# Moving the ones products of gate and branch weights further behind their squares, and one block's squares further behind its load

## The chip, the cores and the metric

The kernel runs on one core of one Trainium2 chip. The metric is the device time of one execution in microseconds (us). Below, PE is the matrix engine, PEld its weight loads, DVE, ACT and POOL the vector, scalar and general engines, SP the engine that issues the transfers. L247 is line 247 of the kernel before.

## What is computed

One layer of an encoder block on x of 1024 tokens by 1024 features, float32 in and out:

```python
u = rms_norm(x, norm1_g)
q, k, v, cb, cc, ch, ga, gb = split(u @ w_in)              # 512 wide each, ga and gb 1024
y_a = neighbourhood_attention(rms(q), rms(k), v, rpb) @ w_attn_branch    # 512 -> 1024
y_b = (cb * conv3(cc * ch, conv_w)) @ w_conv_branch                      # 512 -> 1024
m = sigmoid(ga) * y_a + sigmoid(gb) * y_b
x = x + m @ w_o
h = rms_norm(x, norm2_g) @ w_mlp_in
x = x + square(relu(h)) @ w_mlp_out
```

## The kernel before, in words

**Numbers.** Every float32 matrix is split into two float16 halves, a high part (ACT, a scaled copy) and a low part (DVE, `scalar_tensor_tensor`, the remainder), and a product is made of three matmul passes (high by high, high by low, low by high). Each block of weights is brought to a power of two first, so it needs the sum of squares of the whole block before it can be split.

**How that sum is made.** Four steps on three engines: ACT squares the block and accumulates per partition (L326 for the blocks of `w_attn_branch`, L1411 for the gates, L1434 for `w_conv_branch`; a gate block's halves are multiplied by the norm's gains first, four copies each, L1224); ACT copies the sums into columns of a tile called `ones` (L241, `summed`); PE adds over the partitions with two or four tiny matmuls against a matrix of ones (L247, `all_sum`), called the *ones product* below; DVE turns the result into a power of two (L250, then L518 to L525). After that the split can start (ACT L390 or L1360, DVE L377 or L1364).

**Stages.** The change lies in the stage after attention, 300 to 560 us into the execution. PE works there on *units*: a unit is 12 matmuls of 128x512 into one PSUM bank (6 for the conv branch). The gates ga and gb are made in blocks S1 to S7 by seven products in place of eight (a Strassen-like scheme): seven units each, with weights in the tile `w_s`. Weights A0 to A3 (`w_wa`) and B0 to B3 (`w_wb`) are the four column blocks of the two branch matrices; `ab(j)` is the run of units that multiplies Aj and Bj. The order on PE is: first gate unit, A0, S1, `ab(0)`, S2, S3, `ab(1)`, S4, S5, `ab(2)`, S6, `ab(3)`, S7, then `w_o`. A name in the trace such as `ps_s<-uT,w_s` is a gate unit, `bT,w_wb` a conv branch unit, `qD,w_wa` an attention branch unit.

**What sets the order.** The program is written out by Python generators that run side by side: one emits the PE units, others prepare the coming weight blocks. Each emission of a unit lets the others take some steps. Each engine then runs its own instructions strictly in the order of emission, PE too: a ones product whose column isn't there yet holds up all the units behind it. Two helpers hold a generator back. `apart(mark, n * 6144, work)` waits until n units have been emitted since the mark, so it sets how many units lie between the squares and the ones product. `aged(ch, i, n)` waits until n units after the transfer of a block was issued before the squares are emitted. PSUM banks come from three tags (3 banks d, 3 s, 2 o) by the letters "dsodsods" in turn (`anybank`); the ones products take a bank from the same turn, so a ones product that is moved also changes the bank letters of the units behind it.

**After a gate block.** DVE combines the seven products in PSUM (L1524 to L1546 for one half, L1613 to L1628 for the other), so a bank stays taken until DVE has read it. The four sums of quarter blocks that S blocks need (`gsum`, L1348) are made by POOL, between the combination's own products (L1604). ACT L1493 and L1501 and DVE L1504 turn a finished block of the merged result into its float16 halves.

Of the kernel before, what the change touches and what calls it, by code (L numbers as in the profile page):

```python
# [101 lines left out]
def encoder_block(ctx: ExitStack, tc: tile.TileContext, x, weights, cols, gqk, rel, masks, out):  # L102
# [105 lines left out]
    late, units, forced, side, splitting = [], [0], [False], [False], [False]  # L208
    work, spent, pace = [0], [0], [0]

    def apart(mark, n=3, of=units):
        while of[0] < mark + n and not forced[0]:
            yield WAIT
# [89 lines left out]
    class Chunk:  # L303
# [11 lines left out]
        def prep(self):  # L315
            n = len(self.widths)
            nk = sum(k for k, _ in self.widths)
            rm, a, b, s = (cols_of("prep", i) for i in (nk, 1, 1, 1))
            self.inv = keep()
            tot = sum(k * w for k, w in self.widths)  # L320
            if self.kind == "A" and self is not cA[0]:
                while not self.raw or not aged(self, 0):
                    yield WAIT
                sm = cols_of("prep", 4)
                for i in range(4):
                    A.activation(M[0][:, 7, :256].bitcast(BF16), self.raw[0][:, 256 * i:256 * i + 256], AF.Square,  # L326
                                 scale=sc[:, at(self.rows, i)], accum_out=sc[:, at(sm, i)])
                c = summed(sm)
                yield
                yield from apart(work[0], 3 * 6144, work)  # L330
                yield from all_sum(c, b, anybank(), 1e-36)
                yield from pow2_half(b, 14, s, self.inv)
            elif self.kind in "QKCG":
                self.parts = wsp.tile([128, 2, tot], F16, name="w16_ws", tag="ws")
                for p, (k, w) in enumerate(self.widths):
                    while len(self.raw) <= p:
                        yield WAIT
                    A.activation(self.parts[:, 1, :k * w].bitcast(BF16), self.raw[p][:, :k * w], AF.Square,
                                 accum_out=sc[:, at(rm, p)])
                    yield  # L340
                V.tensor_reduce(sc[:, a], sc[:, at(rm, 0, n)], axis=AX, op=OP.add)
                c = ones_col()
                V.tensor_tensor(c, sc[:, a], sc[:, gm2], op=OP.mult)
                yield from apart(units[0], {"Q": 2, "C": 2, "K": 1}.get(self.kind, 3))
                yield from all_sum(c, b, bank(self.bank) if self.bank else anybank(), 1e-36)
                yield from pow2_half(b, 14, s, self.inv, more=self.more)
            else:
                yield from self.largest(rm, a, b)
                yield from pow2(b, 14, s, self.inv, False, more=self.more)
            V.tensor_scalar(sc[:, rm], sc[:, self.rows], sc[:, s], None, op0=OP.mult)  # L350
            yield
            while done[0] < self.first or self.tag not in wpool:
                yield WAIT
            if self.half is not None:
                if not self.half:
                    vhome.append(wsp.tile([128, 2, 2, tot], F16, name="w16_v", tag="ws"))
                self.parts = vhome[0][:, self.half]
            elif self.kind not in "QKCG":
                self.parts = wpool[self.tag].tile([128, 2, tot], F16, name="w16_" + self.tag, tag=self.tag)
            f = o = 0  # L360
            todo = []
            for p, (k, w) in enumerate(self.widths):
                todo.append((p, [(i * w, w, rm.start + o + i) for i in range(k)], f))
                f += k * w
                o += k
            prev, scaled = None, {}
            for it in todo + [None]:
                if prev:
                    p, parts, f = prev
                    if self.fine:  # L370
                        assert not self.pool
                    for o, m, c in [] if self.fine else parts:
                        hi, lo = (self.parts[:, w, f + o:f + o + m] for w in range(2))
                        if p in self.pool:
                            G.tensor_tensor(lo, scaled[p][:, o:o + m], hi, op=OP.subtract)
                        else:
                            V.scalar_tensor_tensor(lo, self.raw[p][:, o:o + m], sc[:, c:c + 1], hi,  # L377
                                                   op0=OP.mult, op1=OP.subtract)
                    done[0] += 1
                    load_upto(done[0] + 5)  # L380
                splitting[0] = True
                if it:
                    p, parts, f = it
                    if p in self.pool:
                        scaled[p] = w1p.tile([128, 1024], F32, name="scaled", bufs=1)
                        for o, m, c in parts:
                            G.tensor_scalar(scaled[p][:, o:o + m], self.raw[p][:, o:o + m], sc[:, c:c + 1], 1.0,
                                            op0=OP.mult, op1=OP.mult)
                    for o, m, c in parts:
                        A.activation(self.parts[:, 0, f + o:f + o + m], self.raw[p][:, o:o + m], AF.Copy,  # L390
                                     scale=sc[:, c:c + 1])
                    if self.fine:
                        yield
                        for o, m, c in parts:
                            V.scalar_tensor_tensor(self.parts[:, 1, f + o:f + o + m], self.raw[p][:, o:o + m],
                                                   sc[:, c:c + 1], self.parts[:, 0, f + o:f + o + m],
                                                   op0=OP.mult, op1=OP.subtract)
                            if o + m < self.widths[p][0] * self.widths[p][1]:
                                yield
                prev = it  # L400
                self.split = it is None
                yield
# [32 lines left out]
    for (kind, j), pieces in plan():  # L435
        ch = chunks[kind, j] = Chunk(kind, [(nk, sum(n for _, n in cs)) for _, _, nk, cs in pieces],
                                     {"A": "wa", "B": "wb"}.get(kind, "ws"), rows.get(kind, lambda j: g1)(j),
                                     j if kind == "V" else None, 9 if kind in "VQKCGS" else 0)
        ch.first = len(loads)
        for p, (k, w) in enumerate(ch.widths):  # L440
            ch.offs.append(offset)
            if kind != "X" and (kind, j) != ("1", 0) and (kind, j, p) != ("1", 1, 1):
                loads.append((ch, p))
            offset += 128 * k * w
    cG, cS = chunks["G", 0], {n: chunks["S", n] for n in range(1, 8)}
    cV, cConv, cA, cB, cO, c1, c2, c2x = ([chunks[k, j] for j in range(n)] for k, n in
                                              (("V", 2), ("C", 4), ("A", 4), ("B", 4), ("O", 2),
                                               ("1", 16), ("2", 4), ("X", 4)))
# [756 lines left out]
    def scale_of(am, more, n=3):  # L1205

        a, mark = am
        yield from apart(mark, n * 6144, work)
        b, s, inv = cols_of("prep", 1), cols_of("prep", 1), keep()
        yield from all_sum(a, b, anybank(), 1e-36)  # L1210
        yield from pow2_half(b, 14, s, inv, more)
        return s, inv

    def aged(ch, i):
        return forced[0] or i >= len(ch.when) or work[0] >= ch.when[i] + (4 if ch is cS[2] else 2) * 6144

    def rows_scaled(ch, g):

# [181 lines left out]
    def prep_s(n):  # L1400

        ch = cS[n]
        if n == 1:
            while ch.s is None:
                yield WAIT
            s = ch.s
        else:
            yield from rows_scaled(ch, g1)
            sm = cols_of("prep", 2)
            for i in range(2):  # L1410
                A.activation(M[0][:, 7].bitcast(BF16), ch.raw[i], AF.Square, accum_out=sc[:, at(sm, i)])  # L1411
                yield
            c = summed(sm)
            s, ch.inv = yield from scale_of((c, work[0]), 9, 3)
        while done[0] < ch.first or n > 1 and not cS[n - 1].split or gates[0] < n - 1:
            yield WAIT
        t = w3p.tile([128, 4, 512], F32, name="gsum", bufs=1)
        yield from forms_sum(ch, t, None)
        ch.P = wsp.tile([128, 7, 2, 512], F16, name="w16_s", tag="ws")
        yield from forms_split(ch, t, s, ch.P, n == 1, n > 1)  # L1420
        ch.split = True
# [248 lines left out]
    for j in range(4):  # L1670
        if j < 3:
            n = 2 * j + 1
# [11 lines left out]
        n = 2 * j + 2  # L1684
# [666 lines left out]
```

## Time and profile before

| | |
|---|---|
| median of 3 runs | 1209.42 us (1209.11 to 1210.09) |
| profiled execution | 1211.59 us |
| its span in the trace | 1209.8 us |
| PE busy | 1192.8 us, 99% |
| DVE, ACT, POOL busy | 78%, 65%, 40% |
| chain that ended last | PE 61%, DVE 4%, ACT 2%, DMA 2% |

The profiled execution is 2.2 us above the median and contains 1.8 us outside its span. All times of the trace are microseconds from the start of the span. In a timeline row stand the start, the length, the engine, the line, the operation with output and inputs, the count, and in brackets the idle time before it with what ended it. In a row of windows stand, for each engine, its busy time and number of instructions, then the granted PE clock (PEclk, 1.00 is full), the share of time of the DMA engines and GB/s.

### The profile page before, as it was taken

The page shows a single profiled execution, that of the slowest core. Times are in us where ns is not written, and L with a number is a line of the kernel's source. Part 1 is how long each engine was busy: PE and PEld are TensorE (multiplying, and loading weights), DVE is VectorE, ACT ScalarE, POOL GpSimd, SP SyncE. Part 2 cuts the span into 40 slices and gives each one's busy share as a digit, 9 for nine tenths or more (in the row PEclk, how much of TensorE's full clock was granted, in tenths as well). Part 3 has the DMA queues.
Part 4 walks back from the last instruction along what each step waited for, and adds up shares of the span by engine and source line. Part 5 has one row for each costly group of instructions (what it writes and reads, how often), then busy time and mean ns, then how long its engine had stood idle before and what let it go on. Part 6 is the DMA issues. An engine that isn't in the chain of part 4 may idle for free.

```text
span 1209.8 us, 17188 instructions
## 1 busy us (share of the span) xinstructions
PE 1192.8 (99%) x6267; PEld 575.7 (48%) x6267; DVE 947.9 (78%) x1767; ACT 785.8 (65%) x1278; POOL 480.9 (40%) x314
## 2 busy tenths in 40 slices
PE   8999999999989899999999999999999999999998
PEld 7444444455434344444458444444444444444444
DVE  7987877898777677877888655455448989999998
ACT  8774668778777664436778777677675854746440
POOL 5610020221434440411004765565557562564572
PEclk9999999999989899999999999999999999999999
DMA  7755546687684425325196455345375925435202
GB/s 261 194 157 120 114 98 134 138 159 132 162 278 157 151 76 174 95 97 210 28 173 177 163 191 190 126 164 191 123 269 191 349 104 182 166 109 222 104 36 105
DMA packets 168374, 189.63 MB, mean 157 GB/s; under 512 B 123616, under 2 KB 124128, under 8 KB 164192
## 3 DMA queue, kind: packets, MB, share of 16 engines
q1 hardware_dynamic: 168288, 188.52, 51.7%
q8 instruction: 49, 0.80, 0.3%
q14 instruction: 37, 0.30, 0.1%
HBM read 117.19 MB, written 41.42 MB: 131 GB/s over the span
## 4 chain that ended last, share of the span: by engine, by line
PE 61%; DVE 4%; ACT 2%; DMA 2%; issue 1%; POOL 0%; SPq 0%; DVEq 0%
PE ps_d L256 23%; PE ps_s L256 21%; PE ps_o L256 16%; DMA raw<-in_weights 1%; DVE w_s L1364 1%; DMA x<-in_x 1%; DVE mL L1504 0%; DVE sc L409 0%; ACT raw L1224 0%; ACT mH L326 0%; ACT sg L1535 0%; DVE sc L1701 0%; ACT mH L1411 0%; ACT mL L1493 0%; DVE w_wb L1364 0%
## 5 line engine op out<-in xcount | busy, mean ns | idle before, releaser
L256 PEld LDWEIGHTS <-ops 128*128 128x128 f16 x1356 | 132.4, 98 | 157.3
L256 PEld LDWEIGHTS <-w 128*128 128x128 f16 x1368 | 132.9, 98 | 139.4
L1189 PE MATMUL ps_d<-uT,w_ws 128*128 128x512 f16 x576 | 127.9, 379 | 0.0
L256 PE MATMUL ps_s<-ops 128*128 128x512 f16 (+1 forms) x528 | 119.7, 377 | 0.0
L256 PE MATMUL ps_d<-ops 128*128 128x512 f16 x480 | 110.1, 379 | 0.0
L2172 ACT ACTIVATE ops<-hf,sc 128x2048 f16<-128x2048 f32 x26 | 52.0, 1998 | 84.8 <-PE ps_s L256 37.7
L1348 POOL TENSOR_TENSOR tsum<-raw 128x512 f32<-128x512 f32 x28 | 48.2, 1738 | 139.5 <-DVE v L1800 74.0
L1750 POOL TENSOR_TENSOR as<-as 128x512 f32<-128x512 f32 x60 | 82.9, 1381 | 41.7 <-ACT as L2032 38.2
L256 PEld LDWEIGHTS <-w_s 128*128 128x128 f16 x588 | 57.5, 99 | 69.9 <-issue 4.1
L1189 PEld LDWEIGHTS <-w_ws 128*128 128x128 f16 x576 | 54.5, 98 | 65.2 <-issue 1.0
L256 PE MATMUL ps_d<-u2T,w 128*128 128x512 f16 (+1 forms) x360 | 78.8, 368 | 0.0
L256 PE MATMUL ps_o<-ops 128*128 128x512 f16 (+1 forms) x348 | 78.6, 375 | 0.0
L2174 DVE SCALAR_TENSOR_TENSOR ops<-hf,sc,ops 128x2048 f16<-128x2048 f32 x26 | 73.8, 2837 | 3.2 <-ACT ops L2172 2.2
L256 PE MATMUL ps_o<-u2T,w 128*128 128x512 f16 (+1 forms) x348 | 76.0, 368 | 0.0
L256 PE MATMUL ps_s<-u2x,w 128*128 128x512 f16 (+1 forms) x336 | 74.5, 371 | 0.0
L1224 ACT ACTIVATE raw<-raw,sc 128x256 f32<-128x256 f32 x164 | 67.8, 494 | 1.6 <-DMA raw<-in_weights 1.6
L1377 ACT ACTIVATE w<-raw,sc 128x512 f16<-128x512 f32 (+1 forms) x28 | 24.6, 927 | 51.1 <-DVE sc L524 51.1
L2065 DVE TENSOR_TENSOR as<-ps_s,as 128x512 f32<-128x512 f32 x13 | 9.0, 692 | 57.9 <-ACT as L2084 57.9
L2188 POOL TENSOR_TENSOR raw<-raw 128x1024 f32<-128x1024 f32 x8 | 30.8, 3873 | 37.3 <-DVE ops L2182 37.3
L256 PEld LDWEIGHTS <-mH 128*128 128x128 f16 x304 | 29.6, 98 | 30.8 <-issue 0.3
L2178 ACT ACTIVATE ops<-raw,sc 128x1024 f16<-128x1024 f32 x24 | 26.3, 1139 | 26.7 <-DVE sc L152 19.2
L256 PE MATMUL ps_d<-u2x,w 128*128 128x512 f16 (+1 forms) x204 | 43.0, 360 | 0.0
(444 smaller groups left out, 2717.5 us busy)
## 6 DMA issues: line engine op xcount, KB each, us to landing
raw<-in_weights SPq DMA_DIRECT2D x89, 512.0 KB, 5.6
hs<-as SPq DMA_DIRECT2D x16, 1792.0 KB, 8.1
hf<-hs SPq DMA_DIRECT2D x26, 1024.0 KB, 6.5
bT<-bf SPq DMA_DIRECT2D x28, 512.0 KB, 4.4
w2x<-in_weights SPq DMA_DIRECT2D x16, 512.0 KB, 7.8
raw<-in_weights SPq DMA_DIRECT2D x16, 384.0 KB, 3.7
xt<-in_x SPq DMA_DIRECT2D x8, 512.0 KB, 10.8
gs<-s SPq DMA_DIRECT2D x4, 1024.0 KB, 4.4
```

Source lines behind the costliest of these rows:

```text
L256: T.matmul(ps, l, r, start=a, stop=b)
L1189: T.matmul(ps, l, r, start=a, stop=b)
L1224: A.activation(v, v, AF.Copy, scale=sc[:, at(g, 4 * i + k)])
L1348: G.tensor_tensor(t[:, o], a, b, op=OP.add)
L1364: V.scalar_tensor_tensor(o(1), w, sc[:, get(n)], o(0), op0=OP.mult, op1=OP.subtract)
L1377: A.activation(o(0), w, AF.Copy, scale=sc[:, scale(n)])
L1750: sub.tensor_tensor(z[o], z[a], z[b], op=op)
L2065: V.tensor_tensor(z[5], ps[6], z[4], op=OP.add)
L2172: A.activation(P[:, 1, 0], hf, AF.Copy, scale=sc[:, Rs])
L2174: V.scalar_tensor_tensor(P[:, 1, 1], hf, sc[:, Rs], P[:, 1, 0], op0=OP.mult, op1=OP.subtract)
L2178: A.activation(P[:, 0, 0, 1024 * i2:1024 * i2 + 1024], w[i2], AF.Copy, scale=sc[:, fw])
L2188: G.tensor_tensor(w11[i2], w11[i2], w12[i2], op=OP.add)
```

## The change

Three delays are set anew; no arithmetic is changed.

- `Chunk.prep`, kind A (blocks A1, A2, A3): the squares used to be emitted as soon as the block was loaded; now two units after the load was issued, and for A1 seven units after. The ones product follows six units after the squares in place of three.
- `prep_s` (S2 to S7): the ones product follows the squares by 4, 3, 4, 5, 6 and 6 units in place of 3 for all.
- `aged` gets the number of units as a parameter; other blocks keep 2, and S2 keeps 4. The conv branch (`prep_b`) keeps its distances.

```diff
@@ Chunk.prep
-                while not self.raw or not aged(self, 0):
+                while not self.raw or not aged(self, 0, 7 if self is cA[1] else 2):
                     yield WAIT
...
                 c = summed(sm)
                 yield
-                yield from apart(work[0], 3 * 6144, work)
+                yield from apart(work[0], 6 * 6144, work)
                 yield from all_sum(c, b, anybank(), 1e-36)
...
-    def aged(ch, i):
-        return forced[0] or i >= len(ch.when) or work[0] >= ch.when[i] + (4 if ch is cS[2] else 2) * 6144
+    def aged(ch, i, n=2):
+        return forced[0] or i >= len(ch.when) or work[0] >= ch.when[i] + (4 if ch is cS[2] else n) * 6144
...
@@ prep_s
             c = summed(sm)
-            s, ch.inv = yield from scale_of((c, work[0]), 9, 3)
+            s, ch.inv = yield from scale_of((c, work[0]), 9, {2: 4, 3: 3, 4: 4, 5: 5}.get(n, 6))
```

ACT in S1, before the change: A1's four squares and their copy (L326, L241) stand between the copies of S2's first half (L1224) and the conversion of the conv branch (L966).

```order
L1224 ACTIVATE raw<-raw,sc 128x2x128 x4
L326 ACTIVATE mH,sc<-raw,sc 128x256 x4
L241 ACTIVATE ones<-sc 128x4
L966 ACTIVATE mH<-bT 128x512 x2
L1518 ACTIVATE sg<-raw 128x512
L1515 ACTIVATE sg<-ps_s,sc 128x512
```

The same squares on ACT after the change:

```order
L1411 ACTIVATE mH,sc<-raw 128x1024 x2
L241 ACTIVATE ones<-sc 128x2
L1224 ACTIVATE raw<-raw,sc 128x2x128 x4
L1546 ACTIVATE sg<-ps_s 128x512
L1360 ACTIVATE w_wb<-raw,sc 128x2x128 x4
L326 ACTIVATE mH,sc<-raw,sc 128x256 x4
L241 ACTIVATE ones<-sc 128x4
L1360 ACTIVATE w_s<-raw,sc 128x512
```

A1's squares have moved behind the squares of S2 (L1411 and the first L241) and the second part of B0's split (L1360 to w_wb).

ACT in S2 before the change, where the splits of S3's weights (L1360), the squares of S4 (L1411, L241) and the conversion of the merged block (L1501) meet:

```order
L1546 ACTIVATE sg<-ps_o 128x512
L1360 ACTIVATE w_s<-raw,sc 128x512
L1360 ACTIVATE w_s<-raw,sc 128x2x512
L1411 ACTIVATE mH,sc<-raw 128x1024 x2
L241 ACTIVATE ones<-sc 128x2
L1360 ACTIVATE w_s<-gsum,sc 128x2x512 x2
L1501 ACTIVATE mH<-mH,sc 128x1024
```

The same place on ACT after the change:

```order
L1546 ACTIVATE sg<-ps_o 128x512
L1360 ACTIVATE w_s<-gsum,sc 128x2x512 x2
L1224 ACTIVATE raw<-raw,sc 128x2x128 x4
L1411 ACTIVATE mH,sc<-raw 128x1024 x2
L241 ACTIVATE ones<-sc 128x2
L1501 ACTIVATE mH<-mH,sc 128x1024
```

The copies of S4's second half (L1224), its squares and its copy now stand between the split of the quarter sums (`w_s<-gsum`) and L1501; before, they stood ahead of that split.

PE at S5's ones product, before the change: it stands inside `ab(1)`, between two conv branch units.

```order
L256 LDWEIGHTS w_wb
L256 MATMUL ps_d<-bT,w_wb 128x512
L247 LDWEIGHTS ones
L247 MATMUL ps_s<-ones 128x1
...
L256 LDWEIGHTS w_wb
L256 MATMUL ps_o<-bT,w_wb 128x512
```

And after the change:

```order
L256 LDWEIGHTS w_wa
L256 MATMUL ps_o<-qD,w_wa 128x512
L247 LDWEIGHTS ones
L247 MATMUL ps_d<-ones 128x1
...
L256 LDWEIGHTS w_s
L256 MATMUL ps_s<-uT,w_s 128x512
```

It now stands behind the last unit of `ab(1)` and ahead of the first unit of S4. The other ones products move on PE in the same way: S2's from behind four units of S1 (after the first gate unit) to behind five, A1's from behind the first of them to the end of `ab(0)`'s attention units.

## The prediction

> **What bounds the kernel now.** I read the page first, then the waits of PE, then PE's timeline around each wait, and last the timelines of the engines that end the waits.
>
> ```profile
> PE 1192.8 (99%) x6267; PEld 575.7 (48%) x6267; DVE 947.9 (78%) x1767; ACT 785.8 (65%) x1278; POOL 480.9 (40%) x314
> PE ps_s L247 <- ACT ones L241: 7.3, 2, 3.7
> PE ps_d L247 <- ACT ones L241: 1.8, 1, 1.8
> ```
>
> PE is busy 99% of the span, so a change that leaves its matmuls alone can only win what PE waits, or what it runs at a lower clock. The two largest waits of the list are both for the copies that feed ones products, 9.1 us in three places. The timeline shows the first two:
>
> ```profile
> 326.25 2.75 PE L256 MATMUL ps_s<-uT,w_s 128*128 128x512 f16 x12
> 330.84 0.24 PE L247 MATMUL ps_d<-ones 128*128 128x1 bf16 x4 [1.83 <-ACT ones L241]
> ...
> 336.12 2.75 PE L256 MATMUL ps_d<-uT,w_s 128*128 128x512 f16 x12
> 342.61 0.19 PE L247 MATMUL ps_s<-ones 128*128 128x1 bf16 x2 [3.74 <-ACT ones L241]
> 342.82 5.28 PE L256 MATMUL ps_o<-qD,w_s 128*128 128x512 f16 x12
> ...
> 350.75 2.75 PE L256 MATMUL ps_s<-s4T,w_s 128*128 128x512 f16 x12
> 353.34 1.46 PE L256 MATMUL ps_d<-bT,w_wb 128*128 128x512 f16 x6
> ```
>
> A1's product (x4) stands one unit behind 326.25 and waits 1.83 us; S2's (x2) waits 3.74 us, and the unit behind it lasts 5.28 us. A unit has 2.75 us in its row, but the next starts 2.59 us behind its start (350.75 to 353.34), so I step PE by 2.59 for 12 matmuls and 1.30 for 6, and a wait as the trace counts it begins 0.16 us behind the step. The third wait is S5's product, in the middle of `ab(1)`:
>
> ```profile
> 391.05 2.75 PE L256 MATMUL ps_o<-uT,w_s 128*128 128x512 f16 x12
> ...
> 413.16 1.46 PE L256 MATMUL ps_d<-bT,w_wb 128*128 128x512 f16 x6
> 418.22 0.19 PE L247 MATMUL ps_s<-ones 128*128 128x1 bf16 x2 [3.60 <-ACT ones L241]
> 418.27 2.72 PE L256 MATMUL ps_o<-bT,w_wb 128*128 128x512 f16 x6
> ...
> 426.03 1.46 PE L256 MATMUL ps_o<-bT,w_wb 128*128 128x512 f16 x6
> ```
>
> Between 418.27 and 426.03 stand 7.76 us for two half units and a whole one, 5.18 at the normal step: 2.6 us lost to the clock, on top of the wait. After the second wait it is 350.75 less 342.82, 7.93 for two units of 5.18: 2.75 us. The windows show the clock itself:
>
> ```profile
> 327.90:331.30 3.40, 1.57 (x12) 0.68 (x10) 3.26 (x6) 3.27 (x12) 0.00 (x0) 1.00 0.42 95
> 338.20:341.60 3.40, 0.67 (x4) 0.19 (x2) 2.17 (x7) 3.37 (x8) 1.62 (x2) 1.00 1.05 405
> 341.60:348.40 6.80, 5.76 (x16) 2.08 (x16) 3.70 (x4) 4.60 (x12) 6.45 (x6) 0.50 1.02 378
> 413.30:416.70 3.40, 1.32 (x7) 0.49 (x5) 3.37 (x7) 3.40 (x8) 0.28 (x1) 1.00 1.04 419
> 416.70:423.50 6.80, 5.28 (x15) 1.97 (x15) 1.68 (x8) 4.97 (x8) 5.92 (x5) 0.50 0.53 181
> ```
>
> The first figure behind the comma is PE's busy time, the last but two the clock. Two stretches of 6.8 us ran at 0.50. The 3.4 us ahead of them held 0.67 and 1.32 us of PE work. The 3.4 us around the wait of 1.83 held 1.57 us and nothing dropped. So in this trace the drop lies between 1.57 and 1.32 us of work in such a stretch.
>
> **The change, part by part.**
>
> *A1's product.* It goes behind the attention units of `ab(0)`, and its squares go with it, off ACT's list in S1. With `ab(0)` from 350.7 (below), three half units and two whole ones ahead of it, it stands at 359.8, 29 us later. The 1.83 us go at that place. Its new cover is the work of S2's split and B0's on ACT, ahead of it by then.
>
> *S2's product.* It moves by one unit only: five units behind 326.25 is 339.20. What feeds it is not made earlier:
>
> ```profile
> 336.76 0.22 DVE L1439 TENSOR_SCALAR sc<-sc 128x2 f32<-128x2 f32 x1
> 337.01 1.49 ACT L1360 ACTIVATE w_wb<-raw,sc 128x128 f16<-128x128 f32 x4 [2.02 <-DVE sc L1439]
> 338.41 1.69 ACT L1224 ACTIVATE raw<-raw,sc 128x256 f32<-128x256 f32 x4
> 342.35 0.20 ACT L241 ACTIVATE ones<-sc 128x2 bf16<-128x2 f32 x1
> 330.00:340.00 10.00, 8.03 (x40) 3.59 (x40) 9.76 (x24) 7.95 (x19) 0.17 (x1) 1.00 0.74 238
> ```
>
> ACT idles 2.02 us for DVE L1439, and DVE is busy 9.76 of 10 us there (third pair of figures), with the same instructions in the same order as before. A1's squares taken off ACT therefore only lengthen that idle time; L241 stays at 342.35. PE arrives at 339.2, 339.4 by the row's end, and waits about 3.3 us. I let the clock drop as before. Since one unit more is done ahead of the wait, the rest of S1 ends 2.6 us sooner, `ab(0)` starts at 350.7 and S2 at 365.1 (it was 367.64).
>
> *The squares of S4's second half.* They and their copies move, on ACT, from ahead of the split of the quarter sums to behind it, and so ahead of L1501. Behind L1501 hangs DVE, and behind DVE a PSUM bank:
>
> ```profile
> 366.49 0.69 DVE L1617 TENSOR_TENSOR zb<-ps_s,zb 128x512 f32<-128x512 f32 x1 [1.10 <-PE ps_s L256]
> 369.27 1.42 DVE L1593 SCALAR_TENSOR_TENSOR sg<-zb,sc,sg 128x512 f32<-128x512 f32 x2
> 370.10 1.71 POOL L1604 TENSOR_TENSOR mH<-sg 128x512 f32<-128x512 f32 x1 [10.49 <-DVE sg L1593]
> 382.26 1.15 ACT L1360 ACTIVATE w_s<-gsum,sc 128x1024 f16<-128x1024 f32 x1 [2.48 <-POOL gsum L1348]
> 383.32 1.13 ACT L1501 ACTIVATE mH<-mH,sc 128x1024 f16<-128x1024 f32 x1
> 385.53 1.27 DVE L1504 SCALAR_TENSOR_TENSOR mL<-mH,sc 128x1024 f16<-128x1024 f32 x1
> 388.89 0.69 DVE L1527 TENSOR_TENSOR sg<-ps_d,sg 128x512 f32<-128x512 f32 x1
> ```
>
> The chain runs from L1593 over POOL's products and quarter sums to ACT's last split, L1501, L1504, the four additions to L1527. Before, L1527 read a d bank that nothing waited for. With the letters shifted it reads the o bank that S3's third unit needs next. Working: DVE L1617 no longer waits 1.10 us for PE but for its own list, which now has A1's scale and split in it; I put L1593 at 368.0, 1.3 earlier. The bounds of this are 2.6 earlier (all of PE's gain) and 1.1 later (no gain, and the six small steps of A1's scale put in ahead, each at most the 0.22 us of L1439). The inserted work is 4.05 us: L1224, L1411 and L241 of S2 go from 338.41 to 342.46. L1501 then starts at 383.32 - 1.3 + 4.05 = 386.1, L1504 at 387.1, L1527 ends 4.05 us later (385.53 to 389.58 before) at 391.2. PE is at that unit at 365.1 + 9 x 2.59 + 0.1 = 388.5. It waits 2.5 us (from 388.7, the end of the row) and starts at 391.2, where the row of before has 391.05. The 2.6 us won in S1 are gone: 0.15 lost in all.
>
> *What the clock makes of that wait.* Bounds: nothing (the wait of 1.83 us cost no clock) and 2.64 us (the waits of 3.60 and 3.74). 2.5 us lies about midway between 1.83 and 3.60. The windows say the same: 2.5 us of idle time wholly inside a stretch of 3.4 leaves 0.9 us of work, enough for a drop, but split evenly over two it leaves 2.1 in each, and where the stretches fall is not tied to the program. I take half, 1.3 us.
>
> By the Trainium skill, "TensorE: Matmul & The Clock Gate", HAM oscillation, the rule is no idle gaps over about 3.4 us. By that rule this wait would cost no clock. The two drops here followed waits of 3.74 and 3.60 us, which agrees, but the second was split, with 2.1 us of it in the stretch ahead of the drop, so the trace does not bear out the limit as a length of one gap.
>
> *S5's product.* It goes from the seventh place in `ab(1)` to its end:
>
> ```profile
> 410.04 2.00 ACT L1535 ACTIVATE sg<-sg,sc 128x2048 f32<-128x2048 f32 x1 [7.56 <-DVE sg L1533]
> 417.96 0.20 ACT L241 ACTIVATE ones<-sc 128x2 bf16<-128x2 f32 x1
> ```
>
> From S3's third unit at 391.2 come five units (12.95), 0.1 for A2's product, and `ab(1)` with seven half units and four whole ones (19.4): 423.65. Its copy is ready at 418.1, 5.5 us ahead; the cover is gone only if ACT's 410.04 slips by more than that. So the wait of 3.60 and the 2.64 us of clock go: 6.24 us.
>
> *The other products* (S3, B1, S4, A2, B2 to S7). None of S3's, B1's, S4's or A2's waits over 0.2 us before. Worked through with the shifted starts, S3's copy is at 362.2 with PE at 363.7, B1's at 375.0 against 375.4, S4's at 386.1 against 385.9: up to 0.2 us, which would come off the wait behind it. B0's low part, the cover of `ab(0)`, has its end at 349.2:
>
> ```profile
> 346.00 3.29 DVE L1364 SCALAR_TENSOR_TENSOR w_wb<-raw,sc,w_wb 128x256 f16<-128x256 f32 x4
> 450.00:540.00 90.00, 89.84 (x420) 40.70 (x419) 68.23 (x137) 42.56 (x67) 18.28 (x15) 1.00 0.33 103
> 540.40 7.38 DMA x<-in_x
> ```
>
> From 450 to 540 ACT is busy 42.56 of 90 us, so the later products, one to three units further back, keep their cover; I cost them at nothing. The chain of waits passes at 540.40 to a transfer; it follows PE's last gate unit, so it moves with PE and the gain is not lost there.
>
> **Sum.** -6.24 + 0.15 + 1.3 = -4.8 us. The profiled execution, 1211.59 us (span 1209.8 and 1.8 around it), would become 1206.8; it stands 2.2 us above the median of 1209.42, which becomes 1204.6.
>
> **The rivals.**
>
> *A wait without a drop, always.* Same waits, but 2.5 us never costs clock: -6.1, 1203.3 us. For it speaks that no wait under 3.6 us has cost clock here; against it the 1.32 us of work, in a stretch that dropped. This is also the time that the Trainium skill's rule of 3.4 us gives.
>
> *No wait at S3's third unit.* If L1527 ends at 388.7 or sooner, because the chain is 3.8 us earlier than before in place of 1.3 or ACT makes up the 4.05 us, the 2.6 us of S1 stay: -6.24 - 2.6, 1200.6 us. Against it: POOL's and ACT's rows from 370.10 to 383.32 have hardly a gap that could close.
>
> *The wait grows.* If L1593 comes 1.1 us later than before in place of 1.3 earlier, L1527 ends at 393.6, PE waits 4.9 us and the clock drops, as at 3.60: -6.24 + 2.55 + 2.64 = -1.05, 1208.4 us, no change that can be told. For it speaks that DVE is almost full and that A1's split (waiting for ACT) now stands ahead of L1617.
>
> *Slower: S4's second half is loaded late.* A1's raw weights are held till their split, now about 365.5 in place of 361, and the buffer goes to that half of S4.
>
> ```profile
> raw<-in_weights SPq DMA_DIRECT2D x89, 512.0 KB, 5.6
> ```
>
> It should land at 371; ACT wants it at 382.0. Each us after that delays L1501 and PE by one. With the drop the gain left is 3.4 us, so slower by 0.2% begins at a landing of 388, four times the 5.6 us of the row; 10 us late would be about 1216 us. The row speaks against it.
>
> *That the change does not do what it says* holds for S2's product, in the likeliest case already: its distance grows, its wait stays.
>
> **How the numbers follow.** The likeliest case, a wait of about 2.5 us at S3's third unit that costs some clock, 0.50: 1204.6, its own range 1203.3 to 1206.0. No drop 0.20, no wait 0.12, the grown wait 0.11, the late load 0.07. The range goes from 1200.5 (no wait) to 1207.8 (a wait some 2 us longer) and leaves out the late load and most of the grown wait. 0.2% is 2.4 us, about what a measurement of this kernel can tell from no change: the first three cases are faster, 0.82; the grown wait is the same, 0.11; the late load slower, 0.07.
>
> **What would show it.** Right: no wait at A1's product (four matmuls, behind the attention units of `ab(0)`); S2's product waiting 3.3 us till 342.6, with a unit of some 5 us behind it; S3's third unit waiting 2 to 3 us for DVE L1527 till about 391.2; no wait at S5's product, about 423.7, and PE ahead by some 5 us at `w_o`. Wrong: S2's copy earlier than 342 (then DVE was not the limit); L1501 at 383 or earlier; a wait for a ones copy or for weights in S4 to S7; or ACT waiting for a transfer near 382.

## The result and the profile after

The changed kernel takes 1206.25 us (median of 9 runs, 1205.51 to 1206.69) against 1209.38 us of the kernel before on the same chip (1207.37 to 1211.60); the ratio is 0.9973, with a 95% interval of 0.9963 to 0.9983. So 3.1 us are won, where 4.8 were forecast (1204.6 us, range 1200.5 to 1207.8). The profiled execution took 1206.47 us, its span is 1204.7 us.

The first row of the page:

```profile
PE 1189.0 (99%) x6267; PEld 573.9 (48%) x6267; DVE 952.2 (79%) x1767; ACT 786.8 (65%) x1278; POOL 480.0 (40%) x314
```

PE is busy 3.8 us less with the same 6267 matmuls: fewer of them ran at half clock (the mean granted clock is 0.997, before 0.994). PE's timeline in S1 to S5:

```profile
342.71 0.19 PE L247 MATMUL ps_s<-ones 128*128 128x1 bf16 x2 [3.25 <-DMA bf<-mL]
342.93 4.11 PE L256 MATMUL ps_o<-uT,w_s 128*128 128x512 f16 x12
...
349.47 1.46 PE L256 MATMUL ps_s<-bT,w_wb 128*128 128x512 f16 x6
...
358.53 0.24 PE L247 MATMUL ps_s<-ones 128*128 128x1 bf16 x4
...
376.45 0.19 PE L247 MATMUL ps_d<-ones 128*128 128x1 bf16 x2 [2.07 <-ACT ones L241]
376.51 4.39 PE L256 MATMUL ps_s<-uT,w_s 128*128 128x512 f16 x12
380.73 2.75 PE L256 MATMUL ps_d<-qD,w_s 128*128 128x512 f16 x12
...
391.14 2.75 PE L256 MATMUL ps_o<-uT,w_s 128*128 128x512 f16 x12
...
423.62 0.19 PE L247 MATMUL ps_d<-ones 128*128 128x1 bf16 x2
423.67 2.75 PE L256 MATMUL ps_s<-uT,w_s 128*128 128x512 f16 x12
```

A1's product (four matmuls, now at 358.53) no longer waits. S2's waits 3.25 us till 342.71; the row puts that down to a transfer of a tile that this product doesn't read, and what ended it is ACT's copy, below, which is done at 342.66. S5's doesn't wait, and S4 starts at 423.67, where it was 429.91. New is a wait of 2.07 us at 376.45, at B1's product, with 1.6 us of clock behind it (380.73 less 376.51 is 4.22, not 2.59). S3's third unit starts at 391.14; before it was 391.05. A smaller new wait, 1.31 us at 529 us, is shown further down. What ended these waits, on ACT and DVE:

```profile
342.46 0.20 ACT L241 ACTIVATE ones<-sc 128x2 bf16<-128x2 f32 x1
371.01 1.06 ACT L1493 ACTIVATE mL<-mH 128x1024 bf16<-128x1024 f32 x1 [5.78 <-POOL mH L1604]
372.85 1.76 ACT L1360 ACTIVATE w_s<-raw,sc 128x512 f16<-128x512 f32 x2 [0.69 <-DVE sc L524]
376.20 0.20 ACT L241 ACTIVATE ones<-sc 128x2 bf16<-128x2 f32 x1
385.68 1.13 ACT L1501 ACTIVATE mH<-mH,sc 128x1024 f16<-128x1024 f32 x1
...
390.22 0.69 DVE L1527 TENSOR_TENSOR sg<-ps_o,sg 128x512 f32<-128x512 f32 x1
```

B1's squares now stand behind L1493, which waits for POOL, and behind a split that waits for DVE, so their copy is done at 376.3. L1527, which frees the bank that S3's third unit needs, ends at 390.9.

### The profile page after: what moved, and what is told of

Read it like the earlier page. It is cut to its first block, busy times and chain, and to the rows that moved or that the text cites. A ratio compares the mean times of both kernels' runs of the same rounds, so it can differ in the third digit from the quotient of the medians.

```text
span 1204.7 us, 17191 instructions
## 1 busy us (share of the span) xinstructions
PE 1189.0 (99%) x6267; PEld 573.9 (48%) x6267; DVE 952.2 (79%) x1767; ACT 786.8 (65%) x1278; POOL 480.0 (40%) x314
## 4 chain that ended last, share of the span: by engine, by line
PE 86%; DVE 8%; DMA 3%; ACT 1%; issue 1%; SPq 0%; POOL 0%; DVEq 0%; ACTq 0%
PE ps_d L256 26%; PE ps_s L256 23%; PE ps_o L256 20%; PE ps_d L1189 10%; PE ps_d L767 2%; PE ps_s L767 2%; PE ps_o L1170 1%; PE ps_s L1094 1%; DMA raw<-in_weights 1%; PE ps_d L718 1%; DVE w_s L1364 1%; DMA xt<-in_x 1%; DMA x<-in_x 1%; DMA uT<-u 1%; DVE u L639 1%
## 5 line engine op out<-in xcount | busy, mean ns | idle before, releaser
L1224 ACT ACTIVATE raw<-raw,sc 128x256 f32<-128x256 f32 x164 | 67.9, 494 | 1.6 <-DMA raw<-in_weights 1.6
L2146 POOL TENSOR_TENSOR t<-raw,w2x 128x1024 f32<-128x1024 f32 x6 | 19.1, 3190 | 60.7 <-DMA w2x<-in_weights 60.7
```

The source lines that it names most:

```text
L1224: A.activation(v, v, AF.Copy, scale=sc[:, at(g, 4 * i + k)])
L2146: G.tensor_tensor(T2[:, i], w12[i], w22[i], op=OP.add)
```

## The experiments

Times are medians; the kernel before had 1209.1 to 1210.3 us in the four groups of runs, so that differences of under 1 us between versions of different groups don't rest on the medians alone.

### The kernel before once more

> The kernel before, unchanged, for a second profile. Theory (the profiled execution of before, 2.2 us above its median, lost more clock than most, since where the clock's stretches fall is not tied to the program): the same three waits, but 0.7 to 2.7 us less lost to clock in the units behind S2's and S5's product, and 1209 to 1210 us. Rival (it lost it elsewhere): the same slow units as in the first profile.

Measured: 1209.44 us, ratio 0.9998 (0.9988 to 1.0008). The profiled execution took 1207.7 us, 3.9 less than the first one. Its PE timeline at S5's product:

```profile
416.92 0.19 PE L247 MATMUL ps_s<-ones 128*128 128x1 bf16 x2 [3.62 <-ACT ones L241]
416.97 1.45 PE L256 MATMUL ps_o<-bT,w_wb 128*128 128x512 f16 x6
418.26 1.46 PE L256 MATMUL ps_d<-bT,w_wb 128*128 128x512 f16 x6
419.56 2.75 PE L256 MATMUL ps_s<-qD,w_wa 128*128 128x512 f16 x12
```

The wait is the same, the clock isn't. Behind 3.62 us of waiting the two half units take steps of 1.29 and 1.30: full clock, where the first profile lost 2.6 us. Behind S2's product the same wait of 3.74 us cost 1.7 us of clock, where the first profile lost 2.75. Together that is 3.7 of the 3.9 us between the two profiles. The theory held: the execution that the prediction was worked out on had lost more clock than another one.

### S5's distance alone

```diff
-            s, ch.inv = yield from scale_of((c, work[0]), 9, 3)
+            s, ch.inv = yield from scale_of((c, work[0]), 9, 5 if n == 5 else 3)
```

> The kernel before with one edit: S5's ones product five units behind its squares in place of three. Theory (all of the gain is S5's): the waits at A1's and S2's products stay as before, the one at S5's is gone, S4 starts at 423.7 us, 1205.5 to 1206.7 us, as the whole change. Rival (the gain is made in S1 and S2): less than half of the 3.1 us of the change, 1208 us or more.

Measured: 1208.87 us, ratio 0.9997 (0.9988 to 1.0005). S5's wait is gone, but the timelines of PE and ACT show it again in `ab(2)`:

```profile
472.24 0.19 PE L247 MATMUL ps_s<-ones 128*128 128x1 bf16 x2 [2.88 <-ACT ones L241]
464.06 2.00 ACT L1535 ACTIVATE sg<-sg,sc 128x2048 f32<-128x2048 f32 x1 [4.75 <-DVE sg L1533]
```

It is S6's product. ACT waits for DVE till 464.06 and only then makes S6's squares, while PE now arrives earlier. So neither expectation was right: the gain wasn't made in S1 and S2, it was lost again at S6.

### S5's and S6's distance alone

```diff
-            s, ch.inv = yield from scale_of((c, work[0]), 9, 3)
+            s, ch.inv = yield from scale_of((c, work[0]), 9, {5: 5, 6: 6}.get(n, 3))
```

> The kernel before with two edits: S5's ones product five units behind its squares and S6's six, all else three. Theory (S5's distance gives the change's gain, but only with S6's, whose product otherwise takes the wait over at 472 us; all that the change does to A1, S2, S3 and S4 comes to nothing): no wait at S5's and S6's product, the waits at A1's and S2's as before, and about 1205.1 us (1204.3 to 1206.2), as far as the changed kernel with S7 at three units. Rival (S2's unit is needed too): 1207.5 us or more.

Measured: 1203.85 us, ratio 0.9953 (0.9939 to 0.9966), which is 0.5 us under the expected range and 2.4 us under the whole change. PE waits 1.83 us at A1's and 3.74 us at S2's product as before, and nothing from there to 555 us; S4 starts at 422.18:

```profile
342.28 0.19 PE L247 MATMUL ps_s<-ones 128*128 128x1 bf16 x2 [3.74 <-ACT ones L241]
...
422.18 2.75 PE L256 MATMUL ps_s<-uT,w_s 128*128 128x512 f16 x12
```

Two numbers of the change make all of its gain; the rest of it, as it stands in the change, costs 2.4 us (1206.25 less 1203.85).

### S7's distance put back

```diff
-            s, ch.inv = yield from scale_of((c, work[0]), 9, {2: 4, 3: 3, 4: 4, 5: 5}.get(n, 6))
+            s, ch.inv = yield from scale_of((c, work[0]), 9, {2: 4, 3: 3, 4: 4, 5: 5, 7: 3}.get(n, 6))
```

> The changed kernel with S7's ones product three units behind its squares, as before the change. Theory (the wait of 1.3 us at 529 us, for DVE L419, comes from S7's low parts, which the later product has pushed behind DVE L1613 and beside POOL L1604): the wait shrinks to 0.2 us as before, about 1205.1 us (1204.6 to 1205.7). Rival (that wait is only what is left of PE's gain, DVE being full in that stage): the wait stays at 1 us or more, 1206.2 us.

Measured: 1205.06 us, ratio 0.9955 (0.9942 to 0.9967). First the changed kernel (PE, DVE), then this one (DVE, PE):

```profile
529.04 0.16 PE L247 MATMUL ps_d<-ones 128*128 128x1 bf16 x1 [1.31 <-DVE ones L419]
507.61 3.49 DVE L1364 SCALAR_TENSOR_TENSOR w_s<-gsum,sc,w_s 128x1024 f16<-128x1024 f32 x2
```

```profile
503.28 2.47 DVE L1364 SCALAR_TENSOR_TENSOR w_s<-gsum,sc,w_s 128x1024 f16<-128x1024 f32 x2
526.92 0.16 PE L247 MATMUL ps_d<-ones 128*128 128x1 bf16 x1
```

With six units, the first of S7's last two low parts starts on DVE while POOL L1604 runs (506.65 to 508.83) and takes 2.29 us; the second takes 1.27, and with three units both take 1.28. So the two last 3.49 us in place of 2.47, and what follows them, down to the next ones column (L419), is about 1 us later against PE. With three units the wait is gone, as expected. Six units don't do this everywhere, though: in the version further down with the whole part on A undone, S7's product stands one unit earlier, the two low parts take 2.48 us and the wait for L419 is 0.16 us. The profile of this section's kernel, in S2 and S3, shows the bank wait that the prediction had worked out:

```profile
375.64 0.19 PE L247 MATMUL ps_d<-ones 128*128 128x1 bf16 x2 [2.29 <-ACT ones L241]
...
390.19 2.75 PE L256 MATMUL ps_o<-uT,w_s 128*128 128x512 f16 x12 [1.33 <-DVE sg L1527]
```

Here B1's wait cost no clock, so PE reaches S3's third unit sooner and waits there for L1527.

### B1's product further back, S4's squares later, and both

```diff
-        s, ch.inv = yield from scale_of((c, work[0]), 0, 3 if j else 2)
+        s, ch.inv = yield from scale_of((c, work[0]), 0, 4 if j == 1 else 3 if j else 2)
```

> The changed kernel with one more edit: B1's ones product stands four units behind its squares in place of three. Theory (two limits of equal height stand one behind the other: PE's loss at B1's product, and DVE L1527, which frees the o bank of S3's third unit at 390.9 us): the wait of 2.1 us and the slow unit behind it go, a wait of 2 to 3.5 us of an o unit for DVE L1527 takes their place, S3's third unit starts at 391 again, 1206.2 +/- 0.8 us. Rival (PE's loss at B1's product alone sets the time): S3's third unit starts at 387.5 to 388.5 and the time is 1203 to 1203.7 us.

Measured: 1209.79 us, ratio 1.0004 (0.9994 to 1.0013).

```profile
392.08 5.28 PE L256 MATMUL ps_o<-uT,w_s 128*128 128x512 f16 x12 [3.09 <-DVE sg L1527]
397.15 3.21 PE L256 MATMUL ps_d<-uT,w_s 128*128 128x512 f16 x12
...
534.26 0.16 PE L247 MATMUL ps_d<-ones 128*128 128x1 bf16 x1 [2.65 <-DVE ones L419]
```

B1's wait has turned into one of 3.09 us for L1527, as the theory said in place and size. It lost more clock than the wait it replaced, though (397.15 less 392.08 is 5.07 for 2.59), and the wait for L419 grew. The median missed the expectation by 3.6 us. The profile is of the slowest of the eleven executions (1212.98 us), so it shows these losses at their largest.

```diff
-        return forced[0] or i >= len(ch.when) or work[0] >= ch.when[i] + (4 if ch is cS[2] else n) * 6144
+        return forced[0] or i >= len(ch.when) or work[0] >= ch.when[i] + (4 if ch is cS[2] else 4 if ch is cS[4] else n) * 6144
```

> The changed kernel with one more edit: the copies and squares of S4 wait four units behind the load in place of two, so that ACT runs L1501 ahead of S4's squares. Theory of two limits: DVE L1527 ends about 2.4 us earlier, near 388.5, but the wait at B1's product stays, S3's third unit starts at 391 again, 1206.2 +/- 0.8 us. Rival (DVE's L1527 alone sets the time, B1's wait is only where it shows): S3's third unit starts at 388.5 and the time is about 1203.7 us.

Measured: 1209.41 us, ratio 0.9998 (0.9989 to 1.0006).

```profile
375.98 0.19 PE L247 MATMUL ps_d<-ones 128*128 128x1 bf16 x2 [1.75 <-ACT ones L241]
...
391.57 2.75 PE L256 MATMUL ps_o<-uT,w_s 128*128 128x512 f16 x12
...
408.04 4.16 PE L256 MATMUL ps_o<-qD,w_wa 128*128 128x512 f16 x12 [3.21 <-DVE sg L1527]
```

Up to S3's third unit (391.57, no wait) it went as the theory had it, but the time is 3.2 us above the expected 1206.2. The moved ones products shifted the bank letters again, and the next L1527 now holds the bank of an `ab(1)` unit for 3.21 us.

> Both edits together (B1's ones product four units behind its squares, S4's copies and squares four units behind the load). Theory of two limits: now the S1 gain comes through, S3's third unit starts at 388 to 389, S5's product still has its cover, 1203.7 us (1203.2 to 1204.5). If something else sets that time: 1206.2 us with S3's third unit at 391.

Measured: 1207.64 us, ratio 0.9985 (0.9976 to 0.9994).

```profile
389.85 0.19 PE L247 MATMUL ps_s<-ones 128*128 128x1 bf16 x2 [2.34 <-ACT ones L241]
390.65 4.44 PE L256 MATMUL ps_o<-uT,w_s 128*128 128x512 f16 x12 [0.61 <-DVE sg L1527]
```

The gain does not come through: S4's product, whose squares are later now, waits 2.34 us and L1527 another 0.61, and S3's third unit starts at 390.65. So there are not just two limits. Each edit uncovers a third one, at nearly the same time.

### S2's product behind all of S1

```diff
-            s, ch.inv = yield from scale_of((c, work[0]), 9, {2: 4, 3: 3, 4: 4, 5: 5}.get(n, 6))
+            s, ch.inv = yield from scale_of((c, work[0]), 9, {2: 6, 3: 3, 4: 4, 5: 5}.get(n, 6))
```

> The changed kernel with S2's ones product six units behind its squares in place of four, so behind all of S1. Theory (S2's wait isn't what bounds S1, the low part of B0's weights, DVE L1364, ends at 349.4 whatever PE does): no wait at S2's product, a wait of about 4.5 us at the first conv branch unit for DVE L1364, ab(0) starts at 349.4 to 349.6, and from there at most 1.5 us of clock more is lost: 1205.8 to 1207.7 us. Rival (S2's wait of 3.3 us and its clock are still to be had): 1202 to 1203.5 us.

Measured: 1210.21 us, ratio 1.0005 (0.9995 to 1.0014).

```profile
345.80 1.47 PE L256 MATMUL ps_s<-bT,w_wb 128*128 128x512 f16 x6 [1.50 <-DMA bT<-bf]
...
362.71 0.19 PE L247 MATMUL ps_s<-ones 128*128 128x1 bf16 x2 [1.52 <-ACT ones L241]
364.27 4.22 PE L256 MATMUL ps_o<-uT,w_s 128*128 128x512 f16 x12 [1.38 <-DVE sc L524]
...
391.70 2.75 PE L256 MATMUL ps_o<-uT,w_s 128*128 128x512 f16 x12
...
408.59 4.25 PE L256 MATMUL ps_o<-qD,w_wa 128*128 128x512 f16 x12 [3.63 <-DVE sg L1527]
```

S2's product waits no more, and I had the place of the next wait wrong: `ab(0)` starts at 345.80, long before the 349.4 I had put for B0's low parts. But the 3.7 us won there (349.47 in the changed kernel) are gone by S3 (1.52 and 1.38 of waiting, clock), S3's third unit starts at 391.70, and then the bank of `ab(1)` costs 3.63 us more. S2's wait is not where time is to be had.

### The part on A undone, whole and in half

The whole: `aged(self, 0)` and `apart(work[0], 3 * 6144, work)` in `Chunk.prep` as before the change, the rest as changed.

> The changed kernel with the part on A1 to A3 undone (squares emitted at once, ones product three units behind them); S2 to S7 as changed. Theory (in S1 to S3 the part on A takes away what the part on S2 gives, since it puts A1's chain ahead of DVE L1617 and S4's squares ahead of ACT L1501): A1's product waits 1.8 us again, S2's about 1.3 and without a loss of clock, B1's product and S3's third unit don't wait, S3's third unit starts near 388, about 1203.2 us (1202 to 1204.5). Rival (the part on A is worth its 1.8 us): 1207.5 to 1208.5 us.

Measured: 1202.90 us, ratio 0.9940 (0.9927 to 0.9952).

```profile
331.57 0.24 PE L247 MATMUL ps_d<-ones 128*128 128x1 bf16 x4 [1.83 <-ACT ones L241]
343.34 0.19 PE L247 MATMUL ps_o<-ones 128*128 128x1 bf16 x2 [1.16 <-ACT ones L241]
365.23 0.19 PE L247 MATMUL ps_s<-ones 128*128 128x1 bf16 x2 [2.09 <-ACT ones L241]
365.28 4.41 PE L256 MATMUL ps_o<-uT,w_s 128*128 128x512 f16 x12
383.02 1.13 ACT L1501 ACTIVATE mH<-mH,sc 128x1024 f16<-128x1024 f32 x1
```

L1501 is back at 383.02, B1's product and S3's third unit don't wait, and 3.4 us are won against the change. The waits at A1's and S2's product are as expected; that S3's product would wait 2.09 us and lose clock was not. The next version undoes half of it: `aged(self, 0)` as before, the distance of six units kept.

> The changed kernel with A1's to A3's squares emitted at once, as before, but their ones products six units behind. ACT's order round L1501 is then that of before. Theory (A1's product's wait of 1.8 us costs nothing, since S2's product waits for ACT L241 at 342.4 anyway; the harm of the part on A is the place of the squares alone): no wait at A1's product, 3.2 us at S2's, S3's product waiting less in exchange, no wait for DVE L1527, 1203 us (1202.3 to 1204.2). Rival (A1's wait is worth its 1.8 us): 1200.5 to 1201.5 us. Second rival (the distance of six units does the harm): 1205.5 us or more.

Measured: 1203.07 us, ratio 0.9944 (0.9932 to 0.9957).

```profile
342.77 0.19 PE L247 MATMUL ps_o<-ones 128*128 128x1 bf16 x2 [3.14 <-ACT ones L241]
342.98 2.75 PE L256 MATMUL ps_d<-uT,w_s 128*128 128x512 f16 x12
```

A1's wait of 1.83 us is gone, S2's has grown from 1.16 to 3.14, so the two together are what they were (2.99 and 3.14), and so is the time. So that wait was worth nothing, and the harm, 3.2 us by this one edit, lies in the later place of A's squares. With them at their old place B1's squares are back too, at 364.24 ahead of L1493, where the changed kernel makes them at 374.52 behind it. S3's wait of 2.09 us was tried too, on the version with the whole part on A undone:

```diff
-            s, ch.inv = yield from scale_of((c, work[0]), 9, {2: 4, 3: 3, 4: 4, 5: 5}.get(n, 6))
+            s, ch.inv = yield from scale_of((c, work[0]), 9, {2: 4, 3: 4, 4: 4, 5: 5}.get(n, 6))
```

> The changed kernel with the part on A1 to A3 undone, and S3's ones product four units behind its squares in place of three. Theory (what was left in that version was S3's wait of 2.1 us and 1.7 us of clock behind it; the split of the quarter sums at 384.4 allows S3 to start up to 3.3 us earlier): S3's product doesn't wait, S4 starts 2 to 3.5 us earlier, 1200.3 us (1199.4 to 1201.6). Rival (another limit, a bank or B1's low part, takes it back as in S1 to S3 of the changed kernel): 1202 to 1203.5 us.

Measured: 1203.69 us, ratio 0.9955 (0.9941 to 0.9969), 0.2 us above the rival's range. PE's only wait in S2 and S3 is now:

```profile
367.52 4.43 PE L256 MATMUL ps_d<-qD,w_s 128*128 128x512 f16 x12 [2.47 <-DVE zb L1619]
```

The wait of 2.09 us for ACT has become one of 2.47 us for a bank that DVE L1619 frees, one unit on, and it costs 1.7 us of clock too.

### The version that the runs point to

A's squares as before, S7's distance as before, the rest of the change.

> The changed kernel with A1's to A3's squares emitted at once, as before, and S7's ones product three units behind its squares, as before. Theory (the two harms of the change are separate, 3.2 us by the squares of A1 and 1.2 us by S7's distance): the wait for DVE L419 at 526 us is gone, 1201.9 us (1201.3 to 1202.7), the fastest version here. Rival (another step of DVE's takes its place): 1203.1 us.

Measured: 1202.29 us, ratio 0.9934 (0.9921 to 0.9948), the fastest here. PE's first wait behind attention and the unit behind it:

```profile
342.53 0.19 PE L247 MATMUL ps_o<-ones 128*128 128x1 bf16 x2 [3.14 <-ACT ones L241]
342.75 4.44 PE L256 MATMUL ps_d<-uT,w_s 128*128 128x512 f16 x12
```

The wait for L419 is gone. Both harms can be had back one after the other, 3.2 us (1206.25 less 1203.07) and 0.8 us (1203.07 less 1202.29). For the second the medians alone don't prove it, as the intervals of the two ratios overlap; the trace does, in which the wait of 1.3 us is gone. The time is also 1.6 us under that of S5's and S6's distance alone (1203.85), so what is kept for A, S2 and S4 seems to be worth something together; no run takes these parts singly.

The two rows also stand against those of the version with half of the part on A undone: the same place and the same wait of 3.14 us, there with a unit of 2.75 us behind it and here with one of 4.44. Here the lost clock cost nothing. In both versions S4's first unit starts 94.3 us after the gate unit behind A0 (420.76 less 326.41 there, 420.52 less 326.18 here), since without the lost clock S3's product waits 1.82 us for ACT, and with it not at all.

## Why the prediction was right or wrong

**Sign and range right, the size 1.7 us too large.** Against the profiled execution the forecast was 1206.8 us, and that execution took 1206.47. It was the step from there to the median that failed: I lowered the median by as much as the profiled execution. The 6.24 us at S5's product held 2.64 us of lost clock (2.58 by the prediction's own rows, 7.76 less 5.18), and the second profile of the kernel before shows the same wait without any. The first profile was 2.2 us above the median because of such losses, the profile after only 0.2 us: beside the experiments, executions of the kernel before with a mean granted clock of 0.994, which is that of the first profile, took 1210.9 to 1212.5 us, those with 0.999 took 1207.4 to 1209.0.

**S5's product:** right; 423.62 against 423.65 worked out, no wait. What the prediction didn't see is that this gain hangs on S6's distance: with S5's alone it is lost at 472 us. I had costed S6's at nothing, where it was worth 5.0 us once S5's had moved (1208.87 to 1203.85).

**A1's and S2's products:** right. A1's wait went, S2's stayed, 3.25 us (3.3 forecast) till 342.7, since its copy is made when DVE lets it. The clock cost 1.4 us there (349.47 less 342.93, for 5.18), not the 2.75 of before.

**S3's third unit:** the end of the chain was right (L1527 at 390.9 against 391.2; the unit at 391.14 against 391.2), but in this profile no wait for it shows. The step that failed is B1's product, "375.0 against 375.4". ACT's copy came at 376.3, because B1's squares had moved behind L1493 and POOL, and PE came at 374.2, having lost less clock. The wait of 2.07 us and 1.6 us of clock used up the time in which PE would have waited for the bank. Hence my 1.3 us of clock for that wait did not arise, and the unit's start was not later either. That the start agrees to 0.1 us is therefore partly luck: PE set out 1.2 us earlier than forecast (349.47 against 350.7) and lost that much more on the way, at another place.

**The later products at nothing:** wrong for S7's. Putting it back won 1.2 us in the changed kernel (1206.25 to 1205.06) and 0.8 in the other version. I read the cover from ACT, which is half idle there; the engine that paid was DVE.

**Sum:** in the profiles, -6.24 us at S4's start and 1.15 us given back at 529 us (1.31 us of waiting, where before the product of L419 waited 0.16) make the 5.1 us between the spans. That this is so near the 4.8 of the forecast is luck: the 1.3 us of clock at S3's third unit did not arise, the 1.15 us at 529 us had been put at nothing, and the two nearly cancel.

**The rivals.** That the 2.5 us of waiting never cost clock: its wait took another place, and it did cost clock there in this execution. No wait at S3's third unit: the profile shows none, but not for the reason given. The growing wait and the late load did not occur. The prediction weighed the part on A only as far as S3; that the change would be better without it is in line with its own chain (4.05 us put ahead of L1501), but no number was drawn from that.

**The clock.** I let a wait of 2.5 us lose half of the possible clock, as I couldn't tell where the stretches at half clock would fall. The traces can. In each of the 14 profiles the granted clock changes only at moments that lie whole multiples of 3.41 us apart (in the first one at 341.60, 348.42, 416.69 and 423.52: 2, 20 and 2 such steps), and this grid lies elsewhere in each execution. The windows below follow it, first in the second profile of the kernel before, around S5's wait of 3.62 us, then around S2's wait of 3.14 us in the version with half of the part on A undone, then around the same wait in the version behind it:

```profile
411.68:415.09 3.41, 1.62 (x8) 0.64 (x7) 3.38 (x7) 3.41 (x8) 0.00 (x0) 1.00 1.01 410
415.09:418.50 3.41, 1.58 (x10) 0.75 (x10) 1.99 (x8) 2.12 (x6) 3.38 (x3) 1.00 0.71 281
```

```profile
337.78:341.19 3.41, 1.85 (x9) 0.74 (x8) 2.52 (x6) 3.41 (x9) 1.12 (x2) 1.00 1.05 404
341.19:344.61 3.42, 1.82 (x10) 0.97 (x10) 0.00 (x0) 3.36 (x10) 3.26 (x5) 1.00 1.06 408
```

```profile
339.66:343.08 3.42, 0.52 (x4) 0.38 (x4) 0.41 (x2) 3.36 (x8) 3.09 (x5) 1.00 1.06 406
343.08:346.49 3.41, 3.41 (x10) 1.18 (x8) 1.86 (x3) 3.08 (x8) 3.41 (x3) 0.50 1.04 389
```

In the first two executions the grid shares the wait between two windows; each keeps over 1.5 us of PE work, and the clock stays at 1.00. In the third one window takes nearly all of it, 0.52 us of work are left, and the next window runs at 0.50. All 14 profiles, cut this way from 8 us on, have no exception: every window at full clock with 1.39 us of PE work or less (there are 20) is followed by one at half clock, every window with 1.47 us or more by one at full clock. So the same wait costs nothing or some 1.7 us by where the grid lies, and the 1.32 to 1.57 us that the prediction read from one trace hold in all.

By the Trainium skill, "TensorE: Matmul & The Clock Gate", HAM oscillation, the rule is no idle gaps over about 3.4 us. As a length of one gap these runs don't bear it out: the wait of 2.07 us above lost 1.6 us, one of 3.14 lost 1.7, and one of 3.62 lost none. The same page, Part 1, says that the activity window runs freely; the traces agree, with a grid that lies elsewhere in each execution.

## What to carry to other kernels

Where one engine's queue waits at several places for others that are themselves full, look for the next place that arrives late before counting a removed wait as won: S5's was worth 0.8 us without S6's (1209.62 to 1208.87, not clear of the noise) and over 5 with it, A1's nothing at all, and to take away the whole of S2's cost 4 us (1206.25 to 1210.21). Read the cover of a delayed step on every engine it uses, not on the emptiest one. And take lost clock out of a profiled execution before its difference is laid on the median; what a wait costs in clock is a chance, set by how it may fall across two windows of the clock, not one figure.

## What the runs showed of the hardware

A wait of the matrix engine has two prices, its length and the clock behind it. The second is not fixed by the length: 0 (behind waits of 3.62, 3.14 and 2.29 us), 1.4 (3.25), 1.6 (2.07), 1.7 (3.14, and 3.74 in the second profile of the kernel before), 2.5 (3.09) and 2.6 us (3.60) in the profiles above. Waits of 1.83 us and less that stood alone lost none; two of 1.52 and 1.38 us, close together, lost 1.5.

What sets it in these traces is a grid of 3.41 us windows. A window at full clock with 1.39 us of PE work or less was followed by half clock, one with 1.47 us or more was not. Half clock lasted one window (3.41 us) where PE was busy for 2.88 us of it or more, two (6.83 us) in the three cases where it held 2.58 us of work or less.

Two executions of the kernel before differ by 3.9 us, more than the change is worth, and 3.7 us of that is lost clock.

A DVE `scalar_tensor_tensor` of 128x1024 float32 that started while POOL ran a product took 2.29 us, where the next one took 1.27.
